# Channel mixes that copy a pair's first product into a PSUM bank set apart and let TensorE add the second to it

## The chip, the cores and the metric

The program runs on one core of a Trainium2 chip. The metric is the device time of one execution in microseconds (us), the median of three runs. Its engines carry the names of the profile: PE (TensorE, matmuls), DVE (VectorE), ACT (ScalarE), POOL (GpSimd) and SP (SyncE, which issues most loads of weights).

## What is computed

The reference is a trunk of two layers over 512 frames of 1024 channels. Each layer has two recurrent branches, a merge, a channel mix and an embedding term; only the channel mix matters here:

```python
x = x + relu(rmsnorm(x) @ W1 + b1)**2 @ W2 + b2     # W1: 1024 x 4096, W2: 4096 x 1024
x = x + sigmoid(rmsnorm(x) @ W_pg) * (p[i] @ W_pe)
```

## The kernel before, in words

**Number format.** Activations lie transposed, channels on the 128 partitions and the 512 frames in the free dimension. Every fp32 operand is split into a high and a low half: ACT copies the value into the high half (line 309), DVE subtracts it to get the low half (line 310). A product of two split operands is three matmuls: high by high (L539), high by low (L540), low by high (L541).

**Weights.** SP loads raw weights into a ring of four tiles `wr`; `split` turns each into the two halves of a tile `w`. A weight piece is ready when both ACT and DVE have had it, so each of the two engines has a share of every weight.

**Pairs.** Most products of the channel mix use a scheme with seven products of quarter blocks in place of eight. `run_pair` does one unit of 256 output columns. It runs the products in the order P1, P5, then P4 of the pair before (it is put off by `later` and `flush`), P6, P2, P3, P7. Each is 12 matmuls of 128x256. Piece A of the weights serves P1 and P5, piece B serves P2 and P6, piece C serves P3 and P7, and a half-size piece D serves P4. Three PSUM banks take the results: bank a takes P1, and then P6, P7 and P4 are accumulated on top of it; bank c takes P5 and later, started afresh, P3; bank b takes P2 alone. After each product `done` is called with the bank, and each consumer reads it out, before the next product overwrites or extends that bank: P6 can't start until P1 has been read from bank a, and P3 can't start until P5 has been read from bank c. The PSUM pool has 8 banks, all in one ring.

**The two kinds of pair in a channel mix.** The hidden channels are made in 16 tiles `l?fbp` (layer, block b, part p). Some are pairs (5 in layer 0, 9 in layer 1, named in the table FPAIRS), the others use plain matmuls of 128x512. In such a pair `pair_tiles` reads P1 by an ACT copy into SBUF (L612), P5, P6 and P4 also by ACT copies (L614, L618, L624), and P2, P3 and P7 by DVE adds onto what has been copied (L616, L620, L622). The tile is then scaled, put through relu and square (DVE L1494, ACT L1495 and L1496), and made into the operands of the second matmul: a split of three quarters (128x768, names `hh` and `hl`), three DVE instructions for sums (L631, L632, L633), and a split of those (128x1024). P1, P2 and P4 read the quarters; P5, P6, P3 and P7 the sums.

The second matmul runs as 16 pairs per layer, `l?obp`, block b of the hidden channels into part p of the output. Their results go straight onto `x` in SBUF by `add`, all on DVE: P1 and P2 each add to one quarter of x, P5 and P7 to the second, P6 and P3 to the third, P4 to the last (L1532; the first to touch a quarter in block 0 adds the bias too, L1530). So each of these pairs has seven DVE instructions of 128x256.

**The order of the work.** The Tile scheduler puts the instructions of an engine into one order, by priority and dependence; what `ahead()` wraps is put 250 places forward. Tiles of the hidden channels and output pairs alternate: f00 to f03, f10, o00 to o03, f11 to f13, f20, o10 to o13, f21 to f23, f30, o20 to o23, f31 to f33, o30 to o33. POOL builds the sums of weights that the pairs need and writes them back to memory, paced by PE's matmuls; `wr<-s26t` in the trace is such a load.

Of the kernel before, what the change touches and what calls it, by code (L numbers as in the profile page):

```python
# [35 lines left out]
F32 = mybir.dt.float32  # L36
F32R = mybir.dt.float32r
AF = mybir.ActivationFunctionType
# [4 lines left out]
P = 128  # L43
T = 512
# [7 lines left out]
S = 256  # L52
UN = 1024
LOOK = 2
AHEAD = 250
# [198 lines left out]
def build(ctx, tc, ins, out):  # L254
    nc = tc.nc
    ve, ac, gp, te = nc.vector, nc.scalar, nc.gpsimd, nc.tensor
# [3 lines left out]
    def pool(name, bufs, **kw):  # L260
        return ctx.enter_context(tc.tile_pool(name=name, bufs=bufs, **kw))
# [8 lines left out]
    wpool = pool("w", PIECES)  # L270
    bpool = pool("big", 1)
    opool = pool("one", 1)
    psum = pool("ps", 8, space=bass.MemoryType.PSUM)
    cur = {}

    xs_dram = tc.dram_tile([KT, P, T], F32, name="x_spill")
# [22 lines left out]
    nhalf = cpool.tile([P, NT], F32, name="nhalf")  # L299
    gp.memset(nhalf, -0.5)  # L300

    def ps(name):
        return psum.tile([P, T], F32, name=name, tag="ps")

    def tmp(name, dt=F32):
# [74 lines left out]
    def next_unit():  # L380
        n = at["unit"]
        at["unit"] += 1
        tick("FULL" if full(n) and units[n][0] == "PAIR" else units[n][0])
        return n
# [130 lines left out]
    def flush():  # L515

        while later:
            later.pop()()

    def run_pair(name, act, done):  # L520

        n = next_unit()
        assert units[n][0] == "PAIR", units[n]
        bank = {}

        def product(x):
            w, half, j = PRODUCTS[x]
            ready(place[n, "A"] + READY[x])
            wh, wl = [a[:, half * Q:(half + 1) * Q] for a in pieces[n, w]]
            b = {"P2": "b", "P5": "c", "P3": "c"}.get(x, "a")  # L530
            first = x in ("P1", "P2", "P5")
            if first:
                bank[b] = ps(f"{name}{b}")
            o = bank[b][:, 0:S]
            for k in range(4):
                s = slice(k * P, (k + 1) * P)
                h, l = act[k](j)
                f, e = first and k == 0, k == 3
                te.matmul(o, wh[:, s], h, start=f, stop=False, skip_group_check=True)  # L539
                te.matmul(o, wh[:, s], l, start=False, stop=False, skip_group_check=True)  # L540
                cur["mm"] = te.matmul(o, wl[:, s], h, start=False, stop=e, skip_group_check=True)  # L541
            done(x, o)
            pace()

        def last():
            product("P4")
            for w in PIECE:
                del pieces[n, w]

        product("P1")  # L550
        product("P5")
        flush()
        for x in ("P6", "P2", "P3", "P7"):
            product(x)
        later.append(last)
# [34 lines left out]
                then[x, u]()  # L590
            pace()

    def ahead():

        return tc.high_priority(AHEAD)

    def pair_tiles(name, act, consume, y=None, then=None):

        y = y or [tmp(f"{name}y{d}") for d in range(2)]
        a, b = slice(0, S), slice(S, T)  # L600

        def done(x, o):
            with ahead():
                evict(x, o)
            if then and x in then:
                then[x]()
            if x == "P4":
                consume(y)

        def evict(x, o):  # L610
            if x == "P1":
                ac.activation(y[0][:, b], o, AF.Copy)  # L612
            elif x == "P5":
                ac.activation(y[1][:, a], o, AF.Copy)  # L614
            elif x == "P2":
                ve.tensor_tensor(y[0][:, b], o, y[0][:, b], OP.add)  # L616
            elif x == "P6":
                ac.activation(y[1][:, b], o, AF.Copy)  # L618
            elif x == "P3":
                ve.tensor_tensor(y[1][:, b], o, y[1][:, b], OP.add)  # L620
            elif x == "P7":
                ve.tensor_tensor(y[1][:, a], o, y[1][:, a], OP.add)  # L622
            else:
                ac.activation(y[0][:, a], o, AF.Copy)  # L624

        run_pair(name, act, done)
# [336 lines left out]
    x = big("x0", F32)  # L963
# [22 lines left out]
    for i in range(L):  # L986
# [38 lines left out]
        for k in range(KT):  # L1025
            s = slice(k * P, (k + 1) * P)
            f, e = k == 0, k == KT - 1
# [281 lines left out]
        for d in range(4):  # L1309
            o = t8(xa, f"l{i}m0z{d}") if d else oz  # L1310
# [115 lines left out]
        for c in range(KT):  # L1426
# [6 lines left out]
            o = t8(yr, f"l{i}br1{c}")  # L1433
# [13 lines left out]
        if i == L - 1:  # L1447
            x_pool = phase("x", act_side)
            whole = x_pool.tile([P, KT, T], F32, name=f"l{i}x", tag="x")
            x = [whole[:, c, :] for c in range(KT)]  # L1450
        else:
            x = big(f"l{i}x", F32)
# [18 lines left out]
        for c in range(KT):  # L1471
            o = t8((mh, ml), f"l{i}wo{c}")
# [8 lines left out]

        cur["ff"] = cur["tmp"] = phase(f"ff{i}", ph_side)
        cur["ntmp"] = 2
        hid = {}

        def ff1(b, p):
# [70 lines left out]
        first, rest = ff_order()  # L1557
# [19 lines left out]
        def embed(u):  # L1577
            _, wh, wl = unit("PE")
            for c in range(4):
                o = ps(f"l{i}pe{u}{c}")  # L1580
                for k in range(2):
                    s = slice((2 * c + k) * P, (2 * c + k + 1) * P)
                    mm3(o, wh[:, s], wl[:, s], pth[:, k, :], ptl[:, k, :], k == 0, k == 1)
                ac.activation(pe[:, 4 * u + c, :], o, AF.Copy)
                if c == 1:
                    flush()

        embed(0)
        for _, b, p in rest:
            ff2(b, p)  # L1590
        embed(1)
        cur["ff"].release()


# [22 lines left out]
        for c in range(KT - LAST if last else KT):  # L1617
            o = t8(n3.act, f"l{i}pg{c}")
# [44 lines left out]
    for a, n in enumerate(nn):  # L1663
        for c in range(KT - LAST, KT):
            _, wh, wl = ws[c - KT + LAST]
            o = ps(f"pl{a}{c}")[:, :256]
# [141 lines left out]
```

## Time and profile before

| what | value |
|---|---|
| time, median of three runs | 2289.66 us (2287.82 to 2292.54) |
| time of the profiled execution | 2288.05 us |
| its span in the trace | 2286.3 us |
| granted TensorE clock | 0.998 |
| channel mix of layer 0, about | 815 to 1115 us of the span |
| channel mix of layer 1, about | 1930 to 2240 us of the span |

A row of a timeline gives the start, the duration, the engine, the source line, the operation and then output<-inputs with the shape; square brackets hold the idle time ahead of the instruction and what ended it. A row of the waits reads: the waiting group, what it waited for, total us, count, mean us. A row of the windows holds the stretch, its length, and then for PE, PEld (weight loads of the array), DVE, ACT and POOL the busy time and the number of instructions; after these the granted clock, the DMA share and GB/s.

Durations overlap a little on ACT and DVE: an instruction starts before the one ahead of it ends in the listing. A 128x256 matmul is listed with 0.28 us when others follow it, though they start 0.11 us apart. So a gap of the listing is shorter than the time that PE lost: from start to start is the measure.

### The profile page before, as it was taken

To read this page: it belongs to the slowest core of one execution; us is meant where nothing else is said; L and a number is where in the kernel's file an instruction comes from. 1 tells how busy PE (TensorE), PEld (TensorE's weight loads), DVE (VectorE), ACT (ScalarE), POOL (GpSimd) and SP (SyncE) were. 2 spreads that over 40 slices of the span, in tenths; PEclk is the share of its full clock that TensorE was granted. 3 is DMA by queue.
4 is the path that set the end of the run, shared out by engine and by line. 5 is a ranking of instruction groups with operands and counts; after the bars stand their busy time and mean duration, and the time that the engine had idled before them with its cause. 6 is when DMAs were issued, how large, how long until landed. Compare 5 with 4: busy or idle time off the path is not lost.

```text
span 2286.3 us, 36395 instructions
## 1 busy us (share of the span) xinstructions
PE 2266.4 (99%) x13532; PEld 2011.6 (88%) x13532; DVE 1761.6 (77%) x2722; ACT 1265.9 (55%) x1835; POOL 610.0 (27%) x952
## 2 busy tenths in 40 slices
PE   9999999999999999999999999999999999999998
PEld 8888899888898899999888888988888888999997
DVE  7877777886677878778778787778867678787785
ACT  6766544654554546556557564445545446566564
POOL 3332222223124322223532332221231242111112
PEclk9999999999999999999999999999999999999999
DMA  6776887787789888888886768877876888888841
GB/s 214 191 193 175 245 231 220 217 234 213 230 239 267 218 229 233 236 247 221 219 224 182 197 179 249 238 215 225 227 221 213 247 265 218 248 235 229 233 162 56
DMA packets 187890, 499.33 MB, mean 218 GB/s; under 512 B 26352, under 2 KB 29808, under 8 KB 187712
## 3 DMA queue, kind: packets, MB, share of 16 engines
q0 software_dynamic: 57520, 188.53, 36.9%
q1 hardware_dynamic: 114496, 280.97, 36.3%
q10 hardware_dynamic: 15696, 27.50, 3.5%
q8 instruction: 106, 1.74, 0.3%
q14 instruction: 72, 0.59, 0.1%
HBM read 478.03 MB, written 194.51 MB: 294 GB/s over the span
## 4 chain that ended last, share of the span: by engine, by line
PE 87%; DVE 7%; ACT 2%; issue 2%; DMA 2%; POOL 0%; SPq 0%; DVEq 0%; ACTq 0%; POOLq 0%
PE l1br L488 1%; PE l0br L489 1%; PE l0br L488 1%; PE l1br L489 1%; PE l0br L490 1%; PE l1br L490 1%; PE l0f L488 1%; PE l0f L490 1%; PE l0f L489 1%; DVE w_B L310 1%; DVE w_C L310 1%; PE l1f L488 1%; PE l0pg L488 1%; PE l1f L490 1%; PE l1bm L488 1%
## 5 line engine op out<-in xcount | busy, mean ns | idle before, releaser
L309 ACT ACTIVATE w<-wr 128x1024 fp32r<-128x1024 f32 (+1 forms) x193 | 199.7, 1041 | 124.7 <-issue 28.5
L310 DVE TENSOR_TENSOR w<-wr,w 128x1024 fp32r<-128x1024 f32 (+1 forms) x193 | 234.1, 1216 | 43.7 <-ACT w L309 42.8
L309 ACT ACTIVATE w_B<-wr 128x1024 fp32r<-128x1024 f32 x123 | 130.4, 1060 | 148.8 <-PE l1bm L490 13.1
L310 DVE TENSOR_TENSOR w_B<-wr,w_B 128x1024 fp32r<-128x1024 f32 x123 | 150.2, 1222 | 54.3 <-ACT w_B L309 53.8
L309 ACT ACTIVATE w_C<-wr 128x1024 fp32r<-128x1024 f32 x75 | 79.3, 1058 | 65.0 <-issue 6.8
L310 DVE TENSOR_TENSOR w_C<-wr,w_C 128x1024 fp32r<-128x1024 f32 x75 | 92.5, 1233 | 25.6 <-ACT w_C L309 24.7
L310 DVE TENSOR_TENSOR w_A<-wr,w_A 128x1024 fp32r<-128x1024 f32 x75 | 91.7, 1223 | 13.7 <-ACT w_A L309 9.6
L309 ACT ACTIVATE w_A<-wr 128x1024 fp32r<-128x1024 f32 x75 | 79.1, 1054 | 41.2 <-DMA wr<-wpairs 4.4
L309 ACT ACTIVATE w_t<-wr 128x1024 fp32r<-128x1024 f32 x56 | 59.4, 1060 | 64.1 <-PE l1g2va L585 6.3
L309 ACT ACTIVATE w_D<-wr 128x512 fp32r<-128x512 f32 x75 | 47.3, 631 | 81.8 <-DVE wr L470 27.4
L310 DVE TENSOR_TENSOR w_t<-wr,w_t 128x1024 fp32r<-128x1024 f32 x56 | 68.3, 1222 | 21.3 <-ACT w_t L309 20.7
L488 PE MATMUL l0f<-l0n2h,w 128*128 128x512 f32 x176 | 68.7, 390 | 0.0
L489 PE MATMUL l0f<-l0n2l,w 128*128 128x512 f32 x176 | 68.6, 390 | 0.0
L490 PE MATMUL l0f<-l0n2h,w 128*128 128x512 f32 x176 | 68.5, 389 | 0.0
L310 DVE TENSOR_TENSOR w_D<-wr,w_D 128x512 fp32r<-128x512 f32 x75 | 51.7, 690 | 15.0 <-ACT w_D L309 14.5
L367 POOL DMA_DIRECT2D s30t<-wpairs x24 | 16.8, 701 | 92.3 <-PE l1o10a L541 9.2
L490 PEld LDWEIGHTS l0f<-l0n2h,w 128*128 128x128 f32 x176 | 33.0, 188 | 7.0
L488 PEld LDWEIGHTS l0f<-l0n2h,w 128*128 128x128 f32 x176 | 33.0, 188 | 6.6
L489 PEld LDWEIGHTS l0f<-l0n2l,w 128*128 128x128 f32 x176 | 33.0, 188 | 6.5
L488 PE MATMUL l1f<-l1n2h,w 128*128 128x512 f32 x96 | 37.6, 391 | 0.0
L489 PE MATMUL l1f<-l1n2l,w 128*128 128x512 f32 x96 | 37.4, 390 | 0.0
L490 PE MATMUL l1f<-l1n2h,w 128*128 128x512 f32 x96 | 37.4, 389 | 0.0
(5796 smaller groups left out, 9080.3 us busy)
## 6 DMA issues: line engine op xcount, KB each, us to landing
wr<-wstream SPq DMA_DIRECT2D x189, 512.0 KB, 4.8
wr<-wpairs SPq DMA_DIRECT2D x225, 256.0 KB, 4.0
wr<-wwide SPq DMA_DIRECT2D x48, 512.0 KB, 4.5
s3t<-wwide POOLq DMA_DIRECT2D x24, 256.0 KB, 4.7
s6t<-wwide POOLq DMA_DIRECT2D x24, 256.0 KB, 5.2
s18t<-wwide POOLq DMA_DIRECT2D x24, 256.0 KB, 5.5
s21t<-wwide POOLq DMA_DIRECT2D x24, 256.0 KB, 5.0
s24t<-wpairs POOLq DMA_DIRECT2D x24, 256.0 KB, 6.3
```

The costliest lines, as they stand in the source:

```text
L309: a = ac.activation(hi_ap, src, AF.Copy)
L310: return a, ve.tensor_sub(lo_ap, src, hi_ap.bitcast(F32))
L367: dma = gp.dma_start(piece(g, x, p, q), piece(g, MADE[x][a], p, q), max_dma_last_dim=4096, **kw)
L488: te.matmul(o, sh, mh, start=first, stop=False)
L489: te.matmul(o, sh, ml, start=False, stop=False)
L490: cur["mm"] = te.matmul(o, sl, mh, start=False, stop=last)
```

## The change

The PSUM ring is cut to seven banks, and the eighth becomes a pool of its own (`pso`). Outside the channel mixes, every eighth request for a bank is served from that pool, so all eight are used there. In the channel mixes the ring of seven serves all requests but one kind: bank b of each pair is the bank set apart. In the first pair of each layer (o00 in layer 0, f02 in layer 1) P2 starts that bank by itself, as before. In every later pair ACT copies P1 from bank a into it, PSUM to PSUM (128x256, at high priority), in place of the consumer's reading of P1; P2's matmuls are then accumulated on top of the copy, and the consumer reads the sum P1+P2 once, after P2. Layer 0 has 20 such pairs (15 output pairs and 5 tiles), layer 1 has 25 (16 and 9). In an output pair two DVE adds become one. In a tile's pair the ACT copy of P1 to SBUF and the DVE add of P2 become one ACT copy of the sum. In all, DVE has 45 instructions fewer and ACT 45 more.

```diff
-    psum = pool("ps", 8, space=bass.MemoryType.PSUM)
+    psum = pool("ps", 7, space=bass.MemoryType.PSUM)
+    psum_own = pool("pso", 1, space=bass.MemoryType.PSUM)
...
+    cur["own"], cur["turn"] = None, 0
+    def own(name):
+        return psum_own.tile([P, T], F32, name=name, tag="pso")
     def ps(name):
+        if not cur["own"]:
+            cur["turn"] += 1
+            if cur["turn"] % 8 == 0:
+                return own(name)
         return psum.tile([P, T], F32, name=name, tag="ps")
...  (run_pair, product)
-            first = x in ("P1", "P2", "P5")
+            first = x in ("P1", "P5") or x == "P2" and "b" not in bank
             if first:
-                bank[b] = ps(f"{name}{b}")
+                bank[b] = own(f"{name}{b}") if x == "P2" and cur["own"] else ps(f"{name}{b}")
...
-            done(x, o)
+            if x == "P1" and cur["own"] == "written":
+                bank["b"] = own(f"{name}b")
+                with ahead():
+                    ac.activation(bank["b"][:, 0:S], o, AF.Copy)
+            else:
+                done(x, o)
+            if x == "P2" and cur["own"]:
+                cur["own"] = "written"
...  (pair_tiles, evict)
-            if x == "P1":
+            if x == "P1" or x == "P2" and cur["own"] == "written":
                 ac.activation(y[0][:, b], o, AF.Copy)
...  (the channel mix: cur["own"] = "new" at its start, None at its end)
```

Since lines are added, the numbers of the changed kernel are higher by 12 to 20: L309 and L310 become L321 and L322, L539 to L541 become L555 to L557, L1532 becomes L1552, L631 to L633 become L650 to L652, L620, L622 and L624 become L639, L641 and L643, L1494 to L1496 become L1514 to L1516. The copy of P1 is L561. L616 is gone, and the ACT copy of the sum of a tile's pair is L631.

The scheduler also places other instructions differently. DVE at pair o10 of layer 0, where P6 of that pair is the next on PE; `l0f20st` is a tile of hidden channels being finished, `l0x` is x. Before:

```order
L310 TENSOR_TENSOR l0hl_8749<-l0f13st,l0hh_8748 128x1024
L1494 TENSOR_TENSOR l0f20st<-l0f_8929,l0n2rb 128x512
L310 TENSOR_TENSOR w_B<-wr_8838,w_B 128x1024
L1532 TENSOR_TENSOR l0x_7205<-l0x_7205,l0o10a 128x256
L631 TENSOR_TENSOR l0f20st<-l0f20st 128x512
L470 TENSOR_TENSOR wr_8838<-wr_8838 128x512
L310 TENSOR_TENSOR l0hl_8858<-l0f20st,l0hh_8857 128x768
```

And after:

```order
L322 TENSOR_TENSOR l0hl_8752<-l0f13st,l0hh_8751 128x1024
L1514 TENSOR_TENSOR l0f20st<-l0f_8932,l0n2rb 128x512
L322 TENSOR_TENSOR w_B<-wr_8841,w_B 128x1024
L482 TENSOR_TENSOR wr_8841<-wr_8841 128x512
L650 TENSOR_TENSOR l0f20st<-l0f20st 128x512
L322 TENSOR_TENSOR l0hl_8861<-l0f20st,l0hh_8860 128x768
```

The add of P1 onto x, fourth before, is gone, and the sum of two raw halves of a weight (L470, now L482) stands ahead of the sums of f20.

ACT at pair o10 of layer 1; `l1hh` of `l1f13st` are the high halves of the last tile of hidden channels that this pair needs. Before:

```order
L1496 ACTIVATE l1f13st<-l1f13st 128x512
L309 ACTIVATE w_C<-wr_20337 128x1024
L309 ACTIVATE l1hh_20224<-l1f13st 128x768
L309 ACTIVATE l1hh_20224<-l1f13st 128x1024
L309 ACTIVATE w_B<-wr_20358 128x1024
L624 ACTIVATE l1f20st<-l1f20a 128x256
```

And after:

```order
L1516 ACTIVATE l1f13st<-l1f13st 128x512
L631 ACTIVATE l1f20st<-l1f20b 128x256
L321 ACTIVATE l1hh_20227<-l1f13st 128x768
L321 ACTIVATE w_C<-wr_20340 128x1024
L321 ACTIVATE w_B<-wr_20362 128x1024
L321 ACTIVATE l1hh_20227<-l1f13st 128x1024
L561 ACTIVATE l1o10b<-l1o10a 128x256
```

The quarters' split has moved ahead of w_C, the sums' split behind w_C and w_B, and the reading of f20's P2 and the copy of o10's P1 are new here.

PE issues the same instructions, and its order is the same but for a few places. At pair o10 of layer 1, before:

```order
L539 MATMUL l1o10c<-l1hh_20224,w_A 128x256
L540 MATMUL l1o10c<-l1hl_20225,w_A 128x256
L541 MATMUL l1o10c<-l1hh_20224,w_A 128x256
L539 MATMUL l1f20a<-l1n2h_18593,w_D 128x256
L540 MATMUL l1f20a<-l1n2l_18594,w_D 128x256
```

And after:

```order
L557 MATMUL l1f20a<-l1n2h_18608,w_D 128x256
L555 MATMUL l1o10a<-l1hh_19400,w_B 128x256
L556 MATMUL l1o10a<-l1hl_19401,w_B 128x256
L556 MATMUL l1o10c<-l1hl_20228,w_A 128x256
L557 MATMUL l1o10c<-l1hh_20227,w_A 128x256
L557 MATMUL l1o10a<-l1hh_19400,w_B 128x256
```

The last two matmuls of P5, which need the low and high sums of f13, now stand behind P4 of f20 and the first two matmuls of P6. The same has happened at pair o20 of layer 1. POOL and SP keep their orders.

More of the change, by code (lines that the diff above doesn't have):

```diff
@@ L518, in flush, with ahead @@
             later.pop()()
+    def ahead():
+        return tc.high_priority(AHEAD)
     def run_pair(name, act, done):
@@ L591, in run_wide @@
             pace()
-    def ahead():
-        return tc.high_priority(AHEAD)
     def pair_tiles(name, act, consume, y=None, then=None):
@@ L1483, in build @@
         cur["ntmp"] = 2
+        cur["own"] = "new"
         hid = {}
@@ L1591, in build @@
         embed(1)
+        cur["own"] = None
         cur["ff"].release()
```

## The prediction

> **What bounds the kernel now.** The page's first part says which engine to look at:
>
> ```profile
> PE 2266.4 (99%) x13532; PEld 2011.6 (88%) x13532; DVE 1761.6 (77%) x2722; ACT 1265.9 (55%) x1835; POOL 610.0 (27%) x952
> ```
>
> PE is busy 99% of the span, and the change leaves it the same matmuls. So nothing is gained but time in which PE stands. How much of that lies where the change acts, the windows of the two channel mixes say:
>
> ```profile
> 815.00:1115.00 300.00, 297.83 (x2180) 279.66 (x2180) 240.55 (x359) 169.57 (x223) 77.99 (x112) 1.00 0.84 233
> 1930.00:2240.00 310.00, 304.46 (x2369) 290.71 (x2368) 249.32 (x368) 188.18 (x257) 45.15 (x62) 1.00 0.74 216
> ```
>
> PE's listed idle time is 300 − 297.83 = 2.17 us in layer 0 and 310 − 304.46 = 5.54 us in layer 1, 7.7 together. A listed matmul lasts 0.28 us while the next starts 0.11 later, so a pause shorter than 0.17 isn't listed, and each listed one is about 0.16 too short. I counted some 45 pauses from start to start, so the loss is at most 7.7 + 45 × 0.16 = 14.9 us, 0.65% of the time: **the ceiling of any gain**. DVE and ACT are busy 80% and 57% in the first window (240.55 and 169.57 of 300), so DVE is the tighter helper, and DVE is what the change relieves. Third, PE's waits in the stretch of output pairs of each layer say who makes PE stand:
>
> ```profile
> PE l0o10a L539 <- DVE l0x L1532: 0.7, 1, 0.7
> PE l0o20a L539 <- DVE l0x L1532: 0.7, 1, 0.7
> PE l0o30a L541 <- DVE w_B L310: 0.3, 1, 0.3
> PE l0o00a L539 <- DVE l0x L1530: 0.2, 1, 0.2
> ```
>
> ```profile
> PE l1o20a L539 <- DVE l1x L1532: 1.2, 1, 1.2
> PE l1f10a L541 <- DVE w_B L310: 0.8, 1, 0.8
> PE l1o10a L540 <- DVE l1hl L310: 0.6, 1, 0.6
> PE l1o32a L539 <- DVE l1x L1532: 0.5, 1, 0.5
> PE l1o00a L539 <- DVE l1x L1532: 0.5, 1, 0.5
> PE l1o10a L539 <- ACT l1hh L309: 0.4, 1, 0.4
> PE l1o20a L540 <- DVE l1hl L310: 0.3, 1, 0.3
> PE l1o30a L541 <- DVE w_B L310: 0.3, 1, 0.3
> ```
>
> The waits sit in the first pair of each block (o00, o10, o20, o30), where the last hidden tile is being finished while the pair's weights are split; o11 to o13 and o21 to o23 have none. So of the 45 DVE instructions removed, only the few queued ahead of such a wait can pay.
>
> **The change part by part: the adds removed (31 on x, 14 in tiles).** Pair o10 of layer 0 is the clearest. DVE around it:
>
> ```profile
> 888.77 0.69 DVE L631 TENSOR_TENSOR l0f13st<-l0f13st 128x512 f32<-128x512 f32 x1 [1.45 <-ACT l0f13st L1496]
> 889.38 0.68 DVE L1494 TENSOR_TENSOR l0f20st<-l0f,l0n2rb 128x512 f32<-128x512 f32 x1
> 895.60 1.22 DVE L310 TENSOR_TENSOR w_B<-wr,w_B 128x1024 fp32r<-128x1024 f32 x1
> 896.73 0.42 DVE L1532 TENSOR_TENSOR l0x<-l0x,l0o10a 128x256 f32<-128x256 f32 x1
> 900.49 0.41 DVE L1532 TENSOR_TENSOR l0x<-l0x,l0o10c 128x256 f32<-128x256 f32 x1
> 900.82 1.22 DVE L310 TENSOR_TENSOR w_A<-wr,w_A 128x1024 fp32r<-128x1024 f32 x1
> ```
>
> and PE: P1's last matmul, P5's last, P6's first, the last of o11's P5 that still stands ahead of P3, and P3's first.
>
> ```profile
> 894.99 0.28 PE L541 MATMUL l0o10a<-l0hh,w_A 128*128 128x256 f32 x1
> 896.35 0.28 PE L541 MATMUL l0o10c<-l0hh,w_A 128*128 128x256 f32 x1
> 897.29 0.36 PE L539 MATMUL l0o10a<-l0hh,w_B 128*128 128x256 f32 x1 [0.67 <-DVE l0x L1532]
> 900.56 0.28 PE L540 MATMUL l0o11c<-l0hl,w_A 128*128 128x256 f32 x1
> 900.96 0.39 PE L539 MATMUL l0o10c<-l0hh,w_C 128*128 128x256 f32 x1
> ```
>
> P1 ends at 895.27 (894.99 + 0.28). Its add has to wait for w_B's low halves on DVE, ends at 897.15, and P6 starts at 897.29, though P5's last matmul began at 896.35 and P6 could have followed at 896.46: 0.83 us lost. P3 then starts at 900.96, 0.29 late, behind the add of P5 (c), which ends at 900.90 at the end of an unbroken DVE queue. In the new order the add at 896.73 is gone and a 128x256 step is worth 0.33 from start to start (900.49 to 900.82). Moreover f20's scaling, another 128x512 and worth 0.6 from start to start (888.77 to 889.38), now falls in the 1.45 us that DVE idled before 888.77. I replayed the new order by hand with the old durations: w_B ends some 0.35 earlier, at about 896.4, so P6 need not wait; and the add of P5 ends at about 900.35 in place of 900.90. P6's gain is overtaken by P3, which waits on the same queue: what stays is the later one's, about 0.55 (0.33 if only the add counts). Pair o20 of layer 0 shows the same two waits: 0.55 again. At o30 of both layers P6 waits for w_B behind the add of P1: 0.33 each. At o01 of layer 1, where P6 follows P1's add too closely, 0.25.
>
> **The places where the order changed.** In layer 1's o10 both helpers are late:
>
> ```profile
> 2022.05 1.07 ACT L309 ACTIVATE w_C<-wr 128x1024 fp32r<-128x1024 f32 x1 [0.85 <-DMA wr<-s26t]
> 2023.02 1.77 ACT L309 ACTIVATE l1hh<-l1f13st 128x768 fp32r<-128x768 f32 x2
> 2024.70 1.05 ACT L309 ACTIVATE w_B<-wr 128x1024 fp32r<-128x1024 f32 x1
> ```
>
> ```profile
> 2023.88 0.96 DVE L310 TENSOR_TENSOR l1hl<-l1f13st,l1hh 128x768 fp32r<-128x768 f32 x1 [0.82 <-ACT l1hh L309]
> 2025.09 1.21 DVE L310 TENSOR_TENSOR l1hl<-l1f13st,l1hh 128x1024 fp32r<-128x1024 f32 x1
> 2026.22 1.22 DVE L310 TENSOR_TENSOR w_C<-wr,w_C 128x1024 fp32r<-128x1024 f32 x1
> 2036.87 0.38 PE L539 MATMUL l1o10a<-l1hh,w_D 128*128 128x256 f32 x1
> ```
>
> ACT stood 0.85 us for the load of w_C with the quarters' split behind it, and P1 waited for both halves of those quarters (0.4 and 0.6 us in the list above). Now the quarters go ahead of w_C, so their low halves end about 1.2 earlier (2023.6 for 2023.88 + 0.96 = 2024.84) and P1 waits no more. The price: the sums' split stands behind w_C and w_B, one more 1.13 us slot of DVE (2025.09 to 2026.22) behind w_B; P5's last two matmuls wait there about 1 us, now parked behind P4 and two of P6. In the replay P4 of o10 starts at 2036.2 where it was 2036.87, and the next P6 about 0.95 earlier: I take 0.95. This counts on w_B's raw load being in SBUF before 2023.8; ACT took it up at 2024.70 only because it was busy. Had it arrived just then, the gain is 0.3. At o20 the first half of the pair gives nothing (the same trade); its second half waits for P7's add:
>
> ```profile
> 2118.07 0.41 DVE L1532 TENSOR_TENSOR l1x<-l1x,l1o20a 128x256 f32<-128x256 f32 x1
> 2118.54 0.39 PE L539 MATMUL l1o20a<-l1hh,w_D 128*128 128x256 f32 x1 [1.17 <-DVE l1x L1532]
> ```
>
> With two steps fewer ahead of it (P1's add here, and the next pair's) that add ends 0.57 earlier by the replay, and the next wait in the chain gives 0.3: 0.85 (nothing to 0.85). The waits at f10, o00 and o32 have no removed instruction in the queue ahead of them: 0.
>
> **The copies added (45 on ACT).** No copy into PSUM is in the trace; the nearest rows are an ACT copy of a product into SBUF, and, far off, a copy of 128x1024 with 1.07 us (above). Here the former, and what PE did beside another such copy:
>
> ```profile
> 2014.38 0.38 ACT L612 ACTIVATE l1f20st<-l1f20a 128x256 f32<-128x256 f32 x1 [0.29 <-PE l1f20a L541]
> 2019.56 0.37 ACT L618 ACTIVATE l1f20st<-l1f20a 128x256 f32<-128x256 f32 x1
> 2019.73 0.28 PE L540 MATMUL l1f20c<-l1nsl,w_C 128*128 128x256 f32 x1
> 2019.84 0.28 PE L541 MATMUL l1f20c<-l1nsh,w_C 128*128 128x256 f32 x1
> ```
>
> I take 0.38, the same shape from the same memory, and it costs nothing: from P1's end to P6's start lie P5 and P4 of the pair before, 24 matmuls of 0.11 or 2.6 us; in o10 of layer 0, where no P4 is due, 1.2 us (895.27 to 896.46). Without that cover P6 starts late by what the copy ends late: at 1.07 us that is still covered, unless ACT is in a 1.06 us split when P1 ends, which is why o10 of layer 0 might lose up to 0.9. The tiles' new ACT copy of P1+P2 takes the place of one; nobody waits for it directly. ACT's 45 × 0.38 = 17 us go into 45% of idle time. The Trainium skill, ScalarE: Activation LUTs, in its section Step-by-step: what each stage is for, says that ACT reaches PSUM faster than SBUF; no row here shows it, and a shorter copy would leave this term at nothing.
>
> **Seven banks and one.** Each pair holds banks a, b, c and the one of the pair before. Bank b is now the same bank in every pair, written by the copy after P1; it has to be read out before:
>
> ```profile
> 910.66 0.42 DVE L1532 TENSOR_TENSOR l0x<-l0x,l0o11b 128x256 f32<-128x256 f32 x1
> ```
>
> It is free at 911.08, and P3, P7, P1 of the next pair, 36 matmuls of 0.11 or 4 us, stand between P2 and the next copy: no wait, so 0. Outside the mixes the requests take the same turns of eight: 0.
>
> **The sum.** 2 × 0.55 + 2 × 0.33 + 0.25 + 0.95 + 0.85 = 3.8 us. The profiled execution took 2288.05 us (its span is 2286.3, the other 1.75 lie around it), so it would be 2284.25. The median of the runs shown is 1.6 higher, 2289.66, and becomes **2285.9**. With the low ends (0.33 for each of five, 0.25, 0.3, 0) it is 2.2 us, with 2287.5.
>
> **The rivals.** What a measurement can tell from no change is 0.2%, 4.6 us: faster begins below 2285.1, slower above 2294.2.
>
> *The relief carries further.* DVE's queue is lighter by 45 × 0.33 = 15 us in all, tiles are read out sooner, and places that I gave nothing (f10, o32, the short pauses) shrink too. Against it: those waits hang on loads or on DVE work of the same pair. At most 14.9 us; half of it, 7.4, gives 2282.3. Chance 0.18.
>
> *The waits only move.* P6 is early and P3 takes it up, raw loads that PE's progress paces come no sooner, and P5 of o10 and o20 in layer 1, whose operands now come behind two weights, waits as long as P1 did. Then the gain is 0 to 1.5 us: about 2289. For it speaks that P3 already takes a third of P6's gain in layer 0. Chance 0.17.
>
> *Slower: ACT's writes into PSUM hold PE up.* If PE can't write its bank while ACT writes another, PE loses up to 0.38 us per copy: 45 × 0.38 − 3.8 = +13.3, or 2303; with half of that, 2294.4. It decides from 3.8 / 45 = 0.085 us per copy on. Against it: PE kept its 0.11 step while ACT read PSUM (2019.73 to 2019.84, above); but the write is untested. The Trainium skill, PSUM — Partial Sum Buffer, in its section PSUM bank collisions raise a hardware error, says that banks are separate memories and that the chip doesn't stall on a clash; by that rule this rival falls, and the reading row agrees with it, while no run so far shows a write. Chance 0.07.
>
> *Slower: one bank for all P2 serialises the pairs.* A copy that waits for the P1+P2 of the pair before, or a P5 that finds no free bank of the seven, would delay P6; 0.2 us in each of 45 pairs is 9 − 3.8 = +5.2, or 2294.9. Against it: the 4 us of slack above. The Trainium skill, Perfetto Trace Analysis, in its section Matmul Optimizations, advises to use all eight banks; by that rule the time is this rival's, and no row here shows PE waiting for a free bank. Chance 0.05.
>
> **How the numbers follow.** My forecast, a gain of 1.5 to 6 us, has the remaining 0.53. The range takes that, the rival without gain and most of the first, and reaches up towards the two slower ones because the ACT copy's price is not in the trace: 2280 to 2292. Faster by over 0.2% needs 4.6 us: a quarter of the forecast's chance and all of the first rival's, 0.32; slower both last rivals', nearly 0.1; within 0.2% the rest, 0.58.
>
> **What would show it.** Right: in the waits of the profile after, `l0o10a` and `l0o20a` no longer wait for `l0x`, P1 of `l1o10` no longer waits for `l1hl`, `l1o20a` waits 0.6 or less for `l1x`, and PE's listed idle time is nearer to 5 us than 7.7 in the two mixes; the copy takes 0.3 to 0.4, and matmuls beside it keep 0.11. Wrong: new waits of P6 or P2 for ACT's copy, waits of P5 of more than 1 us in o10 or o20 of layer 1, or matmul steps over 0.11 beside the copies.

## The result and the profile after

The changed kernel takes 2284.70 us (median of 17 runs, 2283.36 to 2287.60) where the kernel before took 2288.46 beside it (17 runs, 2286.05 to 2292.54): a ratio of 0.9983, 95% interval 0.9976 to 0.9990, or 3.8 us less. Two more comparisons of the same two kernels, further down, gave 0.9971 (0.9960 to 0.9983) and 0.9991 (0.9982 to 1.0000).

The profiled execution of the changed kernel has a span of 2282.9 us, 3.4 below that of before. First the page's engines, then the windows of the two mixes:

```profile
PE 2266.7 (99%) x13532; PEld 2013.0 (88%) x13532; DVE 1745.8 (76%) x2677; ACT 1280.3 (56%) x1880; POOL 605.8 (27%) x952
```

```profile
815.00:1115.00 300.00, 297.88 (x2177) 279.90 (x2177) 233.01 (x335) 175.18 (x240) 78.17 (x111) 1.00 0.84 231
1930.00:2240.00 310.00, 308.61 (x2402) 295.89 (x2401) 243.62 (x347) 199.69 (x287) 46.89 (x63) 1.00 0.74 219
```

DVE has the 45 instructions fewer and ACT the 45 more that the change announced, and PE's work is the same. But the listed idle time of PE went from 5.54 to 1.39 us in layer 1 and stood still in layer 0 (2.17 and 2.12). The waits of PE say the same, first layer 0, then layer 1:

```profile
PE l0o10c L555 <- DVE l0x L1552: 0.4, 1, 0.4
PE l0o20c L555 <- DVE l0x L1552: 0.4, 1, 0.4
PE l0o10a L557 <- DVE w_B L322: 0.3, 1, 0.3
PE l0o20a L557 <- DVE w_B L322: 0.3, 1, 0.3
PE l0o30a L557 <- DVE w_B L322: 0.3, 1, 0.3
PE l0o31a L555 <- DVE l0x L1552: 0.2, 1, 0.2
PE l0o00a L555 <- DVE l0x L1550: 0.2, 1, 0.2
```

```profile
PE l1o20c L556 <- DVE l1hl L322: 0.4, 1, 0.4
PE l1f10a L557 <- DVE w_B L322: 0.4, 1, 0.4
PE l1o30a L557 <- DVE w_B L322: 0.4, 1, 0.4
PE l1o10c L556 <- DVE l1hl L322: 0.2, 1, 0.2
```

In layer 0 the wait of 0.7 us for the add of P1 is gone at o10 and o20, but two shorter ones stand in its place: P6's third matmul waits for w_B, and P3 (bank c) waits for the add of P5. In layer 1 the waits of P1 (o10, o20) and of P4 (o00, o20, o32, o33) are gone; o33's is there again in the two later profiles of this kernel.

Two numbers are used from here on, both worked out from the start times of all matmuls of the pairs in the two mixes. **Pauses** are what the steps between starts have over 0.114 us, where a step is at least 0.06 over. **The slow step** is what is lost in stretches whose 128x256 matmuls follow each other by about 0.117 us in place of 0.1135; it is told in the last section, with a third, rarer step of 0.120 that this number leaves out (0.3 us or less in these five executions). By execution:

| kernel | pauses layer 0, layer 1 | slow step in the mixes | span |
|---|---|---|---|
| before | 4.6, 10.2 | 1.7 | 2286.3 |
| before, second profile | 4.6, 8.5 | 5.1 | 2288.0 |
| changed | 4.8, 2.8 | 3.9 | 2282.9 |
| changed, second profile | 5.9, 3.5 | 4.2 | 2283.9 |
| changed, third profile | 4.4, 3.3 | 7.6 | 2287.8 |

### The profile page after: what moved, and what is told of

The parts are those of the page before. It is cut to its first block, busy times and chain, and to the rows that moved or that the text cites. A ratio compares the mean times of both kernels' runs of the same rounds, so it can differ in the third digit from the quotient of the medians.

```text
span 2282.9 us, 36390 instructions
## 1 busy us (share of the span) xinstructions
PE 2266.7 (99%) x13532; PEld 2013.0 (88%) x13532; DVE 1745.8 (76%) x2677; ACT 1280.3 (56%) x1880; POOL 605.8 (27%) x952
## 4 chain that ended last, share of the span: by engine, by line
PE 94%; DVE 3%; ACT 1%; DMA 1%; issue 1%; POOL 0%; SPq 0%; DVEq 0%; ACTq 0%; POOLq 0%
PE l0f L500 2%; PE l0f L501 2%; PE l0f L502 2%; PE l1br L500 1%; PE l1br L501 1%; PE l0br L500 1%; PE l0br L501 1%; PE l0br L502 1%; PE l1br L502 1%; PE l1f L500 1%; PE l1f L502 1%; PE l1f L501 1%; DVE w_B L322 1%; PE l0pg L500 1%; PE l1bm L501 1%
## 5 line engine op out<-in xcount | busy, mean ns | idle before, releaser
L322 DVE TENSOR_TENSOR w<-wr,w 128x1024 fp32r<-128x1024 f32 (+1 forms) x193 | 234.5, 1218 | 46.2 <-ACT w L321 44.0
L321 ACT ACTIVATE w<-wr 128x1024 fp32r<-128x1024 f32 (+1 forms) x193 | 199.7, 1041 | 120.3 <-issue 28.5
L321 ACT ACTIVATE w_B<-wr 128x1024 fp32r<-128x1024 f32 x123 | 130.4, 1060 | 150.7 <-PE l0bm L502 13.1
L322 DVE TENSOR_TENSOR w_B<-wr,w_B 128x1024 fp32r<-128x1024 f32 x123 | 150.0, 1221 | 53.0 <-ACT w_B L321 52.5
L321 ACT ACTIVATE w_C<-wr 128x1024 fp32r<-128x1024 f32 x75 | 79.3, 1057 | 61.2 <-issue 9.2
L322 DVE TENSOR_TENSOR w_C<-wr,w_C 128x1024 fp32r<-128x1024 f32 x75 | 93.2, 1243 | 26.6 <-ACT w_C L321 26.3
L322 DVE TENSOR_TENSOR w_A<-wr,w_A 128x1024 fp32r<-128x1024 f32 x75 | 91.6, 1221 | 13.4 <-ACT w_A L321 10.1
L321 ACT ACTIVATE w_A<-wr 128x1024 fp32r<-128x1024 f32 x75 | 79.0, 1053 | 39.5 <-DMA wr<-wpairs 8.8
L321 ACT ACTIVATE w_t<-wr 128x1024 fp32r<-128x1024 f32 x56 | 59.4, 1061 | 63.2 <-PE l0g2va L608 6.3
L321 ACT ACTIVATE w_D<-wr 128x512 fp32r<-128x512 f32 x75 | 47.3, 630 | 68.2 <-DVE wr L482 18.9
L322 DVE TENSOR_TENSOR w_t<-wr,w_t 128x1024 fp32r<-128x1024 f32 x56 | 68.2, 1221 | 21.0 <-ACT w_t L321 20.4
L322 DVE TENSOR_TENSOR w_D<-wr,w_D 128x512 fp32r<-128x512 f32 x75 | 51.7, 689 | 16.3 <-ACT w_D L321 16.0
```

The lines of the kernel that those rows point to most:

```text
L321: a = ac.activation(hi_ap, src, AF.Copy)
L322: return a, ve.tensor_sub(lo_ap, src, hi_ap.bitcast(F32))
```

## The experiments

Where a run is said to lie so many us below or above before, the ratio is meant, taken of before's time in the same comparison; the differences of the medians lie up to 1.1 us off these.

**The changed kernel twice more.** No edit. The first:

> The changed kernel once more, unaltered. Counted from start to start of the matmuls, the two profiles put the gain at 7.5 us of pauses in layer 1's mix and none in layer 0's, while stretches of 128x256 matmuls that run at 0.117 us each in place of 0.1135 take back about 2.3 us and the first 10 us of the kernel 1.1. Theory: the pauses belong to the program, so they come again at the same places, within 0.1 us each; the slower step of stretches and the start belong to the execution, so other stretches are slow this time and the time lost in them differs by 0.5 us or more. Rival: the slow step belongs to the new program (for instance to ACT's writes into PSUM), so the same stretches, 982 to 1027 and 1057 to 1075 us above all, are slow again. Time by both about 2284.7.

Measured: 2284.31 us, ratio 0.9971 (0.9960 to 0.9983). The pauses at o10 and o20 of both layers came again within 0.15 us a pair; those of o31 in layer 0 (0.33, now 1.25), f10 and o33 of layer 1 did not. The slow stretches moved: layer 0 lost 0.4 us to them where it had lost 2.2, layer 1 3.8 for 1.7. From 982 to 1027 us this execution had the quick step. So the pauses belong to the program for the most part, and the slow stretches to the execution. The second, in a later comparison:

> The changed kernel unaltered, for comparison on the same chip: 3.5 to 6.5 us below before. Its pauses come within 0.1 us each at o10, o20 and o30 of both layers; the stretches that run at 0.117 us a matmul differ again from those of the other two executions.

Measured: 2286.60 us, ratio 0.9991 (0.9982 to 1.0000), 2281.13 to 2290.85: 2.1 us below before, less than expected. Its pauses are those of the first profile (7.75 us in sum, where that had 7.6), but the profiled execution lost 7.6 us in slow stretches. This is the same program, so the time moves by several us with next to no change in what waits for what.

**Layer 1 alone.**

```diff
-        cur["own"] = "new"
+        cur["own"] = "new" if i == 1 else None
```

> The change in layer 1 alone; layer 0's mix as before, on eight banks in turn. Theory: layer 0 gave nothing, its pauses only moved from P6 to P3, so the whole gain stays: 3 to 5 us below before, with layer 1's waits as in the changed kernel and layer 0's (0.7 us of P6 of o10 and of o20 for the add on x) as before. Rival, the split of the prediction (1.43 us in layer 0, 2.4 in layer 1): some 2.4 us below before.

Measured: 2285.60 us, ratio 0.9980 (0.9971 to 0.9989), 4.6 us below before. Leaving layer 0 as it was gives up nothing: its waits of 0.7 us at o10 and o20 are back, its pauses sum to 4.2 us against 4.8 of the changed kernel. The interval, 2.5 to 6.6 us, holds the theory and ends just above the prediction's split.

**Output pairs alone, and tiles alone.** In the first, the copy is made only for names l?o.., in the second only for l?f..:

```diff
-            if x == "P1" and cur["own"] == "written":
+            if x == "P1" and cur["own"] == "written" and name[2] == "o":     # "f" in the second
...
-            if x == "P1" or x == "P2" and cur["own"] == "written":
+            if x == "P1":                                                   # unchanged in the second
```

> Only the output pairs copy and accumulate (31 adds on x less); a tile's pair reads P1 and P2 as before. The scheduler keeps the old order of ACT at o10 of layer 1 (w_C ahead of the quarters' split). Theory: each part pays at its own places; here the pauses of P4 at o00, o20, o32 and o33 and of o01 in layer 1 go (about 3.5 us), those of P1 at o10 and o20 and of f10 stay: 2 to 4 us below before. Rival: the order that the tiles' part brings about does nearly all, so this kernel is within 1 us of before.

> Only the tiles' pairs copy and accumulate (14 adds of P2 less on DVE, read by ACT in their place); the output pairs keep both adds on x. The scheduler gives ACT at o10 of layer 1 the new order (quarters' split ahead of w_C). Theory: the waits of P1 at o10 and o20 and some of f10's go (about 3 us), those of P4 at o00, o20, o32 and o33 stay: 2 to 4 us below before. Rival: this order does nearly all of the gain, so the time is that of the changed kernel, about 3.8 us below before, and o32 and o33 no longer wait either.

Measured: output pairs alone 2283.33 us, ratio 0.9972 (0.9962 to 0.9982), 6.4 us below before; tiles alone 2288.73, ratio 0.9993 (0.9984 to 1.0002), 1.6 below. Neither theory nor rival had the sizes: the output pairs bring as much as the whole change or more, the tiles little. The waits of the tiles alone show what their part does (layer 1):

```profile
PE l1o20a L555 <- DVE l1x L1552: 0.6, 1, 0.6
PE l1o32a L555 <- DVE l1x L1552: 0.5, 1, 0.5
PE l1o10c L556 <- DVE l1hl L322: 0.4, 1, 0.4
PE l1o20c L556 <- DVE l1hl L322: 0.4, 1, 0.4
```

P1 of o10 and o20 no longer waits, since the scheduler put the quarters' split ahead of w_C; it is P5's parked matmuls (bank c) that wait, 0.4 us each; and P4's waits for DVE's adds on x stay, but for o00's. The output pairs alone were run once more:

> The change in the output pairs alone once more, on the same chip as the other three. It was 6.4 us below before, with the lower part of its interval near the changed kernel's. If the tiles' part loses 1 to 2 us, as the two parts measured one by one let it seem, this is again 5 to 7 us below before, and 1 us or more below the changed kernel; if the two are alike it is about 4 to 5 below before. Its pauses come again within 0.1 us each, and those of layer 0's o10 and o20 are 1.1 us a pair where before had 1.4.

Measured: 2284.17 us, ratio 0.9977 (0.9969 to 0.9986), 5.3 us below before. The pauses of o10 and o20 in layer 0 were 1.08 us a pair, as expected, for 1.4 before. Layer 1's pauses didn't come again within 0.1 us, as was expected: they were 3.9 us in sum where the first profile had 5.4. Its waits in layer 0 and the first of layer 1:

```profile
PE l0o21a L557 <- DVE w_A L322: 0.4, 1, 0.4
PE l0o11a L557 <- DVE w_A L322: 0.4, 1, 0.4
```

```profile
PE l1o30a L557 <- DVE w_B L322: 0.4, 1, 0.4
PE l1o20a L556 <- DVE l1hl L322: 0.3, 1, 0.3
PE l1o10a L556 <- DVE l1hl L322: 0.3, 1, 0.3
```

In layer 0 neither P6 nor P3 of o10 waits any more; the late one is now w_A of the next pair. In layer 1 P1's waits for the low quarters are there (the old order), P4's at o32 and o33 are gone.

**Copies without the removal of adds.** P2 starts its bank afresh, and all readings by the consumers are as before; the copy's result isn't used.

```diff
-            first = x in ("P1", "P5") or x == "P2" and "b" not in bank
-            if first:
+            first = x in ("P1", "P2", "P5")
+            if first and not (x == "P2" and "b" in bank):
...
-            else:
-                done(x, o)
+            done(x, o)
```

> Copies and the bank set apart as in the changed kernel, but the copies are of no use: P2 starts its bank afresh, and DVE has all its adds again (31 on x, 14 in tiles); ACT has 45 copies more than before. Theory: the gain comes from the adds that DVE is rid of, and a copy is hidden, so nothing is gained and little lost: within 2 us of before, and the waits of P4 at o00, o32 and o33 of layer 1 for DVE's adds are back. Rival, the gain comes from the bank set apart and the shifted order: 3 us or more below before. Rival, the copies cost PE time that the removed adds outweigh: 5 us or more above before.

Measured: 2289.50 us, ratio 1.0008 (1.0000 to 1.0017): no gain, 1.8 us slower at the mean. Bank set apart, copies, 45 ACT instructions more, and the time is that of before. The pauses sum to 13.7 us (before had 14.8 and 13.1 in its two profiles). Waits for DVE are back, here some of layer 1; o32's, which was expected among them, is not (0.07 us):

```profile
PE l1o10a L556 <- DVE l1hl L322: 0.7, 1, 0.7
PE l1o20a L556 <- DVE l1hl L322: 0.7, 1, 0.7
...
PE l1o33a L555 <- DVE l1x L1551: 0.5, 1, 0.5
...
PE l1o00a L555 <- DVE l1x L1551: 0.2, 1, 0.2
```

So copies and bank alone gain nothing: the gain is that of the removed adds, together with the order that the scheduler makes of them. The two aren't separated here, since ACT at o10 of layer 1 has neither the old order nor the changed kernel's. What the copies cost is within 2 us or so by the means, and at most 3.9 us by the interval.

**The copy twice**, on top of the output pairs alone.

```diff
                     ac.activation(bank["b"][:, 0:S], o, AF.Copy)
+                    ac.activation(bank["b"][:, 0:S], o, AF.Copy)
```

> The kernel with the change in the output pairs alone, with each P1 copied twice into the bank: 31 ACT copies of 0.37 us more, nothing else. Theory: the copy is hidden behind P5 and P4, so the second one is too: within 1.5 us of the output pairs alone, 4 to 7 us below before; at o10 of layer 0, where the cover is 1.2 us, P6 may wait 0.3 us for it. Rival, ACT's writes into PSUM hold PE up by half their length: 31 x 0.19 = 6 us slower than the output pairs alone, or the time of before.

Measured: 2286.81 us, ratio 0.9991 (0.9982 to 1.0000), where the output pairs alone had 0.9977 in the same comparison: 3.2 us slower, between the two expectations. PE's longest waits in layer 0 are for the second copy:

```profile
PE l0o10a L555 <- ACT l0o10b L562: 1.0, 1, 1.0
PE l0o20a L555 <- ACT l0o20b L562: 1.0, 1, 1.0
```

```profile
898.63 0.37 ACT L561 ACTIVATE l0o10b<-l0o10a 128x256 f32<-128x256 f32 x1
898.93 0.61 ACT L1517 ACTIVATE l0f20st<-l0f20st 128x512 f32<-128x512 f32 x1
899.45 0.36 ACT L562 ACTIVATE l0o10b<-l0o10a 128x256 f32<-128x256 f32 x1
```

The scheduler put a Square between the two copies, so P6, which could have followed P5 at 898.74, waited for the second. At o30 of both layers P6 waits for it, too (0.2 and 0.4 us). Where the cover is P5 and P4 (o11, o12 and so on), there is no wait for a copy. These waits explain little of the 3.2 us: the one at o10 and o20 stands in place of others, 1.23 us a pair where the output pairs alone had 1.08. In sum the pauses are 11.6 us, where the output pairs alone had 9.2 and 7.7, and most of that lies at P4 of o31 in layer 0 and of o00, o32 and o33 in layer 1, which are listed as waiting for adds on x. Why a second copy makes those late is open.

PE isn't held up by the writes themselves; in the changed kernel the matmuls beside a copy keep their step:

```profile
915.86 0.37 ACT L561 ACTIVATE l0o12b<-l0o12a 128x256 f32<-128x256 f32 x1 [0.29 <-PE l0o12a L557]
```

```profile
915.77 0.28 PE L556 MATMUL l0o12c<-l0hl,w_A 128*128 128x256 f32 x1
915.88 0.28 PE L557 MATMUL l0o12c<-l0hh,w_A 128*128 128x256 f32 x1
916.00 0.28 PE L555 MATMUL l0o12c<-l0hh,w_A 128*128 128x256 f32 x1
916.11 0.28 PE L556 MATMUL l0o12c<-l0hl,w_A 128*128 128x256 f32 x1
```

Over all 45 copies of this execution, the steps between matmul starts that lie inside a copy average 0.1140 us (111 steps), and those within 1.5 us of one 0.1143 us (1129 steps).

**Why layer 0 gave nothing, first theory.** f20's scaling is held behind the sums of f13.

```diff
-                ve.tensor_tensor(a, o, n2.b, OP.mult)
+                m = ve.tensor_tensor(a, o, n2.b, OP.mult)
+                if i == 0 and d == 0 and p == 0 and b > 1:
+                    tc.add_manual_dep(m.ins, cur["sum"].ins.name, ORDER, reason="sums first")
```

> The changed kernel with f20's (and f30's) scaling in layer 0 held behind the sums of the tile before it, as DVE had it before the change; all else in the same order. Theory: the forecast gain of layer 0 was lost to this one place, since the scaling waits for PE while the sums are ready; so w_B's low halves come 0.3 to 0.4 us earlier, and the pauses of P6 and P3 at o10 and o20 of layer 0 fall from 1.39 us a pair to 1.0 or less: 0.7 us or more in all, 2284 or below. Rival, the pauses there hang on the loads or on ACT: they stay within 0.1 us of 1.39.

Measured: 2284.71 us, ratio 0.9981 (0.9972 to 0.9990). The pauses at o10 and o20 were 1.54 us a pair (1.44 in the next expectation, which leaves out 0.11 at the start of the next pair), no fewer than in the changed kernel: the theory fell. The sums' first instruction had kept its distance from P4 of f13, so what makes it late lies ahead of it, and ACT's rows show it. ACT of the changed kernel, where the last matmul of f13's P4 starts at 886.77 and ends at 887.05 us, and the sums' first instruction on DVE:

```profile
886.72 0.72 ACT L1515 ACTIVATE l0f13st<-l0f13st,bc 128x512 f32<-128x512 f32 x1 [2.70 <-DVE l0f13st L1514]
887.47 0.63 ACT L1516 ACTIVATE l0f13st<-l0f13st 128x512 f32<-128x512 f32 x1
888.01 0.36 ACT L643 ACTIVATE l0f13st<-l0f13a 128x256 f32<-128x256 f32 x1
```

```profile
890.55 0.69 DVE L650 TENSOR_TENSOR l0f13st<-l0f13st 128x512 f32<-128x512 f32 x1
```

and of the kernel before, where that matmul starts at 885.42 and ends at 885.70, and the sums start at 888.77 (the row stands in the prediction):

```profile
886.22 0.36 ACT L624 ACTIVATE l0f13st<-l0f13a 128x256 f32<-128x256 f32 x1
886.49 0.62 ACT L1496 ACTIVATE l0f13st<-l0f13st 128x512 f32<-128x512 f32 x1
```

The reading of P4 (L624, now L643) follows P4's end by 0.96 us in the changed kernel, behind a Square, and by 0.52 in the kernel before. The sums start 3.50 and 3.07 us after P4. The output pairs alone have the numbers of before, 0.52 and 3.07; the tiles alone those of the changed kernel, so it is the tiles' part that brings the new order about.

**Second theory, tested.** That Square is held behind the reading of P4, in layer 0 alone.

```diff
-                ac.activation(a, a, AF.Square)
+                q = ac.activation(a, a, AF.Square)
+                if i == 0 and d == 1 and p == 3 and (b, p) in FPAIRS[i]:
+                    tc.add_manual_dep(q.ins, cur["p4"].ins.name, ORDER, reason="P4 first")
```

> The changed kernel with one ACT instruction moved at the end of f13 and f23 of layer 0: the copy of P4 goes ahead of the Square of the tile's other half, as before the change. Holding f20's scaling back did nothing (1.44 us a pair in place of 1.39), so that theory fell. New theory: in the changed kernel P4's copy stands behind that Square on ACT, 0.45 us later after P4's end than with the output pairs alone, and the scaling, the sums and w_B's low halves are all late by it. Then with the copy first the sums start 3.1 us after P4's end in place of 3.5, and the pauses of o10 and o20 in layer 0 fall to 1.1 us a pair or less: 0.6 us or more in all. Rival, the delay hangs on the tile's P2 that ACT now reads (L631): 3.5 us and 1.39 stay.

Measured: 2280.87 us (5 runs, 2279.69 to 2284.26), ratio 0.9967 (0.9955 to 0.9980), 7.6 us below before. The sums start 2.84 us after P4, and the pauses at o10 and o20 are 0.89 us a pair for 1.4:

```profile
PE l0o11a L557 <- DVE w_A L322: 0.4, 1, 0.4
PE l0o21a L557 <- DVE w_A L322: 0.4, 1, 0.4
PE l0o30a L557 <- DVE w_B L322: 0.2, 1, 0.2
```

P6 and P3 of o10 and o20 have no listed wait any more. With the one instruction moved, the scheduler also put f20's scaling back behind the sums, and on ACT the split of f13's quarters back ahead of w_C. The first theory's kernel shows that the scaling alone gains nothing; the shares of the Square and of w_C aren't separated. The gain over the changed kernel is more than this place explains (1 us): in sum its pauses, 7.7 us, are no fewer than in the third profile of the changed kernel, since P4 of o20 in layer 1 waits again; but its execution lost 0.6 us to the slow step and some 1.5 us to the third step of 0.120, that one 7.6 us to the slow step. Whether five runs had luck there stays open.

**The output pairs everywhere, the tiles in layer 1 alone.** The condition is `name[1:3] != "0f"`.

> Output pairs copy and accumulate in both layers, tiles' pairs in layer 1 alone. From the pauses of the parts: layer 0's of the output pairs alone (3.8 us), layer 1's of the changed kernel (2.8 to 3.5): 6.6 to 7.3 us in all, where before has 14.8 and the changed kernel 7.5 to 9.3. Theory: the time follows the pauses, so 5 to 8 us below before and 1 to 2 below the changed kernel. Rival: the slower step of stretches after a pause outweighs this, and the two can't be told apart.

Measured: 2283.29 us, ratio 0.9977 (0.9967 to 0.9987), 5.3 us below before. The pauses were 4.2 and 4.7 us, not 6.6 to 7.3 in all: P4 of o20 waits 0.8 us for DVE here, too. It can't be told apart from the output pairs alone.

**The kernel before, once more.**

> The kernel before, unaltered, for a second profile of it. Its pauses in the two mixes were 14.8 us; three profiles of the changed kernel have 7.5, 9.3 and 7.8, so 6.6 us less, while the medians differ by 2 to 5.6 us. Theory: the pauses come again, 14 to 15.5 us, and the rest is the slower step of stretches, 0.117 in place of 0.1135 us a matmul: the changed kernel lost 3.9, 4.2 and 7.6 us to it in the mixes, before 1.6, and before loses less than 4 again. Rival: the slower step falls on both alike, before loses 4 us or more to it this time, and the gap between pauses and medians stays unexplained.

Measured: 2289.69 us, ratio 0.9999 (0.9990 to 1.0008). The pauses were 13.1 us, less than expected (f10 paused 0.5 in place of 1.5), and the slow step cost 5.1 us: the rival's numbers. So the slow step falls on both kernels, and that the change makes it worse isn't shown.

## Why the prediction was right, and where its working wasn't

The forecast of 2285.9 us, 3.8 below before, was measured as 3.8 below before. The direction and the place of the gain, PE's waits for DVE in the first pairs, were forecast for reasons that held in layer 1. But that the number agrees is luck: the sum is right by terms that are wrong on both sides. With the pauses of two profiles of before and three of the changed kernel (means):

| term | forecast gain | measured |
|---|---|---|
| layer 0: o10, o20 | 1.10 | 0.0 |
| layer 0: o30 | 0.33 | 0.1 |
| layer 1: o01, and o00 taken as 0 | 0.25 | 1.1 |
| layer 1: o10 and o11 | 0.95 | 1.7 |
| layer 1: o20 and o21 | 0.85 | 2.2 |
| layer 1: o30 | 0.33 | 0.0 |
| layer 1: f10, o31 to o33 | 0 | 1.2 |
| layer 0: o31 to o33 | 0 | −0.6 |
| outside the mixes | 0 | −1.8 |
| slow step | not a term | −1.9 |

**What bounds the kernel.** Right: PE's pauses in the mixes were what there was to win. The ceiling of 14.9 us is the 14.8 of that execution; the second one had 13.1. The low end of the sum counts 0.33 us for five places where the sum itself has four (o10 and o20 of layer 0, o30 of both layers): it would be 1.9 us, not 2.2.

**The adds removed, layer 0.** "f20's scaling [...] now falls in the 1.45 us that DVE idled" and "w_B ends some 0.35 earlier" is the step that failed. The changed kernel, DVE's split of w_B and the last matmul of P5 at o10:

```profile
897.27 1.22 DVE L322 TENSOR_TENSOR w_B<-wr,w_B 128x1024 fp32r<-128x1024 f32 x1
897.70 0.28 PE L557 MATMUL l0o10c<-l0hh,w_A 128*128 128x256 f32 x1
```

Here w_B's low halves end 0.79 us after P5's last matmul starts (898.49 and 897.70); before, by the rows in the prediction, 0.47 (896.82 and 896.35). They came 0.3 us later in relation to PE, so P6 still paused 0.5 us for 0.83, and P3 0.59 for 0.29: nothing gained. The replay took the new order of DVE at the place, but not that of ACT some ten instructions earlier, where the reading of P4 had moved behind a Square. The sum of the two waits is what the rival "the waits only move" described, and both went when the reading was put back ahead of the Square and the neighbouring orders came back with it. My next theory, f20's scaling, was wrong as well.

**Layer 1, o10 and o20.** The mechanism was right: the quarters go first, P1 waits no more, and P5's two last matmuls take over a shorter wait. It was forecast at about 1 us and measured at 0.35 to 0.59, so the terms were too small. At o20 the second half of the pair (P4 after P7's add) gave its 1.4 us whole in the three profiles, though in three other kernels with the same code in layer 1 that P4 waits 0.3 to 1.0 us.

**Waits put at nothing.** At o00, o32 and o33 of layer 1 I found no removed instruction in the queue ahead and wrote 0. o00 lost its pause in all three profiles, o32 too, o33 in one of three. At o00 the chain goes through ACT, ahead of DVE's last idle gap: before, ACT read f10's P4 1.07 us after its end, behind a Square, and in the changed kernel 0.04 us after. With the tiles alone, where the add of o00's P1 stays, it is 0.04 us too and the pause is gone, so here it is the tiles' part. The queue ahead has to be followed over more than the last idle gap. With the output pairs alone o32's and o33's pauses go, with the tiles alone they stay, which speaks for the adds on x; but o32's went with copies and all adds as well (0.07 us) and stayed with each P1 copied twice (0.79 us), so the cause there isn't shown.

**The copies.** Right: 0.37 us each (forecast 0.38, from the copy into SBUF), and no listed wait is for them. (Layer 1 has ten tiles made as pairs, not nine; the first, f02, gets no copy.) The rival in which ACT's writes hold PE up is refuted by the step of 0.114 inside and beside the copies, and by the kernel with copies and all adds, which is at most 1.0017 of before. The Trainium skill, ScalarE: Activation LUTs, in its section Step-by-step: what each stage is for, says that ACT reaches PSUM faster than SBUF; this trace shows next to no difference: 0.37 us for the copy into PSUM, 0.36 to 0.39 for a reading of the same shape into SBUF.

**Seven banks and one.** Right inside the mixes: no listed wait of the changed kernel is for a free bank. The Trainium skill, Perfetto Trace Analysis, in its section Matmul Optimizations, asks that all eight banks be used; with seven in turn and one set apart they still are, and the price that the rival put on the narrower ring did not show. Outside the mixes the term 0 was too good: the stretch in which the scheduler moved four transposes by some 75 instructions is 0.13 to 0.23 us longer in each layer, in all twelve profiles of kernels with a bank set apart, and the whole outside was 0.8 to 2.7 us slower in the three profiles of the changed kernel, where the two profiles of before agree within 0.1. The rest of that is scattered, the first 30 us among it, and its cause is open.

**What is left open.** Gains in pauses (5.7 us) less the two losses (1.8 and 1.9) give 2.0 us, about the 2.3 us between the mean spans; the medians differ by 2.1, 3.8 and 5.6 us in three comparisons, the two later ones on different chips. The scatter of the slow step is as large as the gain, so how much of it is the change's own isn't settled.

## What to carry to other kernels

An instruction taken off a helper engine pays only where the busy engine waits for what stood behind it; here that is above all the first pair of a group, and the kernel without the 31 adds on x gained as much as the whole change, while that without the other 14 gained 1.6 us, which can't be told apart from nothing. A hand replay has to begin where the new order first differs, on every engine in the chain, and not at the wait: one reading of a bank that moved behind a Square, with the order that came along, undid the gain of a layer. When forecasts and medians agree, the terms should still be compared one by one, since they can cancel.

## What was not expected of the hardware

Back-to-back 128x256 matmuls have two common steps and a rarer third. In the profile of before, and then of the changed kernel, at the same place of the program (P7 of o22 in layer 0):

```profile
1001.95 0.28 PE L539 MATMUL l0o22a<-l0hh,w_C 128*128 128x256 f32 x1
1002.07 0.28 PE L540 MATMUL l0o22a<-l0hl,w_C 128*128 128x256 f32 x1
1002.18 0.28 PE L541 MATMUL l0o22a<-l0hh,w_C 128*128 128x256 f32 x1
1002.29 0.28 PE L539 MATMUL l0o22a<-l0hh,w_C 128*128 128x256 f32 x1
```

```profile
1003.92 0.28 PE L555 MATMUL l0o22a<-l0hh,w_C 128*128 128x256 f32 x1
1004.03 0.28 PE L556 MATMUL l0o22a<-l0hl,w_C 128*128 128x256 f32 x1
1004.15 0.28 PE L557 MATMUL l0o22a<-l0hh,w_C 128*128 128x256 f32 x1
1004.27 0.28 PE L555 MATMUL l0o22a<-l0hh,w_C 128*128 128x256 f32 x1
```

Three steps take 0.34 us in the one and 0.35 in the other; over a product of 12 that is 1.36 and 1.40 us, or 0.1135 and 0.117 a matmul, at a granted clock of 0.998 in both executions. The third is 0.120 us, here in the kernel with P4's reading put back, at a granted clock of 0.998 again; the two rows are twelve matmuls apart:

```profile
1058.03 0.28 PE L555 MATMUL l0o30c<-l0hh,w_C 128*128 128x256 f32 x1
...
1059.47 0.28 PE L555 MATMUL l0o30a<-l0hh,w_C 128*128 128x256 f32 x1
```

A stretch keeps its step until a pause or another shape of matmul comes, and may have another after it: of 243 stretches of at least 36 matmuls in the fourteen profiles, five change within, each at a pause too short to be counted above. The same place had the quick step in the second profile of the changed kernel. By the two slower steps the mixes lost between 0.7 and some 8 us in the fourteen profiles, nearly as much as lies between the fastest and the slowest of these programs: it is large enough to be why one program's runs spread over 5 to 10 us, though that was only argued, and no view of waits shows it, since PE is listed as busy throughout.
